# Where output copies stand in VectorE's queue, and where a norm's factor is applied

## The chip, the cores and the metric

The kernel runs on one core of a Trainium2 chip. The metric is device time in microseconds (us). TensorE multiplies matrices into PSUM, VectorE (DVE) and ScalarE (ACT) do elementwise work and read PSUM, GpSimd (POOL) issues the indirect fetches here, and SyncE (SP) issues the other transfers. Each engine takes its own instructions in order, and engines wait for one another through semaphores.

## The reference, cut to what matters

256 tokens of 1024 channels go through two blocks, in fp32. The first has a convolution, a differential attention and a cross attention; the second has stick-breaking attention and a gated recurrence, and ends in an expert layer. The change touches the seam before that layer, and the layer's end:

```python
h = rms_norm_2(x, norm_ffn)                 # x * rsqrt(mean(x*x) + eps) * g
q = h @ w_query                             # 1024 -> 8 heads x 2 x 128
s = q . sub_keys                            # 128 keys for each half
top_s, top_i = top_k(s, 16)                 # then the best 16 of 16 x 16 sums
g = softmax(best_s);  u, v = expert_u[idx], expert_v[idx]
act = gelu(h . u)
x = x + sum(g * act * v)                    # 16384 experts, 8 x 16 of them for a token
```

## The kernel before, in words

Channels lie on partitions, tokens along the row; activations are tiles of 128 x 8 x 256. The weights of all layers but the experts come as 94 blocks, each in two halves of 128x1024 fp32 (0.524 MB). ACT casts a half to a high part and VectorE subtracts to get a low part, and `linT` adds three products: high weight by high activation, high by low, low by high. Activations are split into a high and a low tile (`split`, or `gain_col`, which multiplies with the gain on the way).

The queries of the expert layer need the normalised residual. Its mean square is summed on TensorE with `rms_sq` as the last parts of the residual `xr` come (L922 to L927); `rstd_of` makes the token's factor `rx` on ACT and VectorE; `rms_cols` (L963) writes `h3f` = xr times gain times factor, column by column, and splits it into `h3`. Eight `linT` (L1066) then make the queries, ACT copies each out of PSUM (L1068), and small products with the keys give the scores. VectorE finds the top 16 in a background list of small steps (`top16`, `decode`, `gates`), which ends with the indices of the rows to gather.

The expert layer is done in two ways. For 160 tokens all 16384 experts are multiplied: the weights u (`u_pair`, L288) and then v (`v_pair`, L1169) stream through, 128 halves each, and one-hot products (L1136, L1147) set the gates in between. The sums y stand in four PSUM tiles `yT` until the end. For the other 96 tokens only the chosen rows are fetched: 96 fetches of 128 rows of u, then 96 of v (`fetch`, L1178, 0.524 MB each), on GpSimd's queue. VectorE multiplies rows of u with the token (`dot`, L1185) and sums rows of v into `acc` (`axpy`, L1203). A fetch needs a free buffer: three of the tag `gat` and five of `gat2`. Fetch `n` takes a `gat` buffer if `n % 8 < 3`. The weights u and v go through a ring of 13 halves on SP's queue (L230).

At the end `rows_out` transposes and adds the gathered tokens' parts (L1229, L1231), copies them out (L1233) into a `gat` buffer and stores them (L1234). For the 160 tokens ACT and VectorE copy `yT` (L1282, L1283) and SP stores it (L1284).

The program is traced in Python, and a planner lays the instructions of each engine in an order by a time model of its own; the code's order is a priority only. `issue_after(x)` lays the instructions in its block behind x in the same engine's queue. The order that came out is that of the profile.

Of the kernel before, what the change touches and what calls it, by code (L numbers as in the profile page):

```python
# [188 lines left out]
def build(tc, xT, memT, vec, con, con0, wcat, rgw, keysT, u, v, urow, vrow, out):  # L189
    nc = tc.nc  # L190
    es = ExitStack()
    with es:
        cpool = es.enter_context(tc.tile_pool(name="const", bufs=1))
        spool = es.enter_context(tc.tile_pool(name="stream", bufs=1))
        ex = ExitStack()
        xpool = ex.enter_context(tc.tile_pool(name="xres", bufs=1))

# [11 lines left out]
        def V(n, i=0, k=1):  # L209
            o, _ = VEC[n]  # L210
            return VT[:, o + i:o + i + k]
# [135 lines left out]
        xr = xpool.tile([P, NC, T], F32, name="xr")  # L347
        rx = xpool.tile([P, T], F32, name="rx")
        cur = {}
# [9 lines left out]
        def statp():  # L359
            return cur["ps"].tile([P, 512], F32, name="stat", tag="stat", bufs=1)  # L360
# [64 lines left out]
        def bc2(r):  # L425
            return r.unsqueeze(1).to_broadcast([P, 2, T])
# [37 lines left out]
        with ExitStack() as e1:  # L464
            big = e1.enter_context(tc.tile_pool(name="big", bufs=11, side="right"))
            cur["sm"] = e1.enter_context(tc.tile_pool(name="sm", bufs=2, side="right"))
# [4 lines left out]
            def bigt(n, dt=F32):  # L471
                return big.tile([P, NC, T], dt, name=n, tag="big")


# [13 lines left out]
            nc.sync.dma_start(ident, con0[:, :P])  # L488
            mgh, mgl = bigt("mgh", F32R), bigt("mgl", F32R)
            for c in range(NC):  # L490
# [109 lines left out]
            qd, kd, vd = bigt("qd"), bigt("kd"), big.tile([P, 2, 1024], F32, name="vd", tag="big")  # L600
            oxh, oxl = bigt("oxh", F32R), bigt("oxl", F32R)
            for j in range(4):
# [63 lines left out]

            odh, odl = bigt("odh", F32R), bigt("odl", F32R)
            for j in range(4):
# [46 lines left out]
            with tc.issue_after(last.ins):  # L715
                for c in range(NC):
                    nc.scalar.activation(cn[:, c], cn[:, c], AF.Silu, bias=V("conv_ln_b", c))
            ch, cl = bigt("ch", F32R), bigt("cl", F32R)
            for j in range(4):
# [10 lines left out]

            h2 = (bigt("h2h", F32R), bigt("h2l", F32R))
            st = statp()
# [185 lines left out]
            hold = state["rstd"]  # L918
            st2 = statp()
            for j in range(2):  # L920
                for k, ps in enumerate(linK(mx, 0, None if j else (scp(), scp()))):
                    sl = slice(4 * j + 2 * k, 4 * j + 2 * k + 2)  # L922
                    g = smt("gate", 512, 3).rearrange("p (a b) -> p a b", a=2)
                    nc.vector.tensor_mul(g, ps, bc2(rsb))  # L924
                    nc.vector.tensor_add(xr[:, sl], xr[:, sl], g)
                    rms_sq(xr, st2, 4 * j + 2 * k, NC)
                state["hold"] = hold  # L927
            rstd_of(st2[:, :T], 1.0 / 1024, T, out=rx)

# [18 lines left out]

        NB, MORE = 3, 5
        xG = rows.tile([P, NC, NG], F32, name="xG")  # L950
# [8 lines left out]
        with ExitStack() as e3:  # L959
            hq = e3.enter_context(tc.tile_pool(name="hq", bufs=1, side="right", reuse_waits="tile"))  # L960
            h3 = [hq.tile([P, NC, T], F32R, name="h3hi"), hq.tile([P, NC, T], F32R, name="h3lo")]
            rms_cols(xr, "norm_ffn_2", *h3, r=rx, full=h3f)
            state["hold"] = state["split"]  # L963
            ex.close()
# [100 lines left out]
            for hd in range(8):  # L1065
                pq = linT(h3, hd == 0)  # L1066
                q = tk.tile([P, 2, T], F32, name="q", bufs=1)
                nc.scalar.copy(q, pq)  # L1068
                pss = gps.tile([P, 512], F32, name="gp", tag="gp").rearrange("p (t h n) -> p t h n", t=2, h=2)
                for t in range(2):  # L1070
                    for p_ in range(2):
                        nc.tensor.matmul(pss[:, t, p_], q[:, p_, t * P:(t + 1) * P], kT[:, 2 * hd + p_],
                                         start=True, stop=True)
                ss = tk.tile([P, 2, 2, P], F32, name="ss", bufs=2)
                nc.scalar.copy(ss, pss)
                for t in range(2):
                    for p_ in range(2):
                        top16(V16[:, t, hd, p_], I16[:, t, hd, p_], ss[:, t, p_], "s2")
                    bg.append((0.0, cands(hd, t)))
                background(2.5)  # L1080
# [91 lines left out]
            def fetch(src, k):  # L1172
                n, box["slot"] = box["slot"], box["slot"] + 1
                if "more" in box and n % (NB + MORE) >= NB:
                    g = box["more"].tile([P, 1024], F32, name="gat2", bufs=MORE)
                else:
                    g = rows.tile([P, 1024], F32, name="gat", tag="gat", bufs=NB)
                nc.gpsimd.indirect_dma_start(g, None, src, bass.IndirectOffsetOnAxis(gi[:, 0, k:k + 1].bitcast(U32), 0))  # L1178
                return g
# [17 lines left out]
            def axpy(k, m, g):  # L1197
                with tc.issue_after(state["dve"].ins):
                    if m not in acc:
                        acc[m] = rows.tile([P, 1024], F32, name=f"acc{m}", tag=f"row{m}")  # L1200
                        nc.vector.tensor_scalar_mul(acc[m], g, cG[:, k:k + 1])
                    else:
                        nc.vector.scalar_tensor_tensor(acc[m], g, cG[:, k:k + 1], acc[m], op0=ALU.mult, op1=ALU.add)  # L1203

            def gathered():

                held = []
                for f, src in ((dot, urow), (axpy, vrow)):
                    for m, (o_, g, _) in enumerate(groups):
                        for k in range(o_, o_ + g):  # L1210
                            if len(held) == NB + ("more" in box) * MORE:
                                fn, *a = held.pop(0)
                                fn(*a)
                            a = (k, hrow[m]) if f is dot else (k, m)
                            held.append((f, *a, fetch(src, k)))
                            weights()
                            yield
                for fn, *a in held:
                    fn(*a)
                yield  # L1220
# [35 lines left out]
        ga.append(g2pool.tile([P, 32, D], F32, name="ga2"))  # L1256
        box["more"] = es.enter_context(tc.tile_pool(name="rows2", bufs=1, side="right", reuse_waits="tile"))
        for g8 in range(D // 8):
# [21 lines left out]
        for b in range(4):  # L1280
            o = ga[0][:, 2 * b:2 * b + 2]
            nc.scalar.copy(o[:, 0], yT[b][:, 0, :D])  # L1282
            nc.vector.tensor_copy(o[:, 1], yT[b][:, 1, :D])  # L1283
            nc.sync.dma_start(yo[:, 2 * b:2 * b + 2], o)  # L1284
# [22 lines left out]
```

## Time and profile before

| | |
|---|---|
| median of 3 runs | 1322.68 us (1321.14 to 1325.76) |
| profiled execution | 1325.82 us, its span 1324.0 us |
| TensorE busy | 1250.4 us, 94% |
| VectorE busy | 937.6 us, 71% |
| ScalarE busy | 456.7 us, 34% |
| GpSimd busy | 218.3 us, 16% |
| moved by DMA | 340.75 MB, mean 257 GB/s |

The span is the time from the first to the last instruction. Busy shares are means over stages with different limits. TensorE's matmuls are pipelined, and a busy TensorE can still be fed slowly.

### The profile page before, as it was taken

How to read it: one execution, taken by the hardware profiler on the slowest of the kernel's cores; microseconds unless marked ns; L12 is line 12 of the kernel's file. 1: busy time of each engine (PE TensorE's matmuls, PEld its weight loads, DVE VectorE, ACT ScalarE, POOL GpSimd, SP SyncE). 2: the span in 40 equal slices, each digit the busy share in tenths (PEclk: the TensorE clock that was granted, in tenths of full speed). 3: DMA queues.
4: the chain of work that ended last, by engine and by line, in shares of the span. 5: the costliest groups of instructions: out<-in, count | busy, mean ns of one | idle time of the engine just before them, and what ended most of it. 6: DMA issues, size and time to landing. Idle time of an engine off the chain costs nothing.

```text
span 1324.0 us, 24472 instructions
## 1 busy us (share of the span) xinstructions
PE 1250.4 (94%) x9948; PEld 1211.4 (91%) x9948; DVE 937.6 (71%) x1806; ACT 456.7 (34%) x733; POOL 218.3 (16%) x222
## 2 busy tenths in 40 slices
PE   8999999999999999998999999999999999999902
PEld 7999999899999999887999999999999999999901
DVE  6799888888997687847998544875547865440095
ACT  7546677668647458845313010000100000000000
POOL 0000000000000000000012532323412253330072
PEclk9999999999999999999999999999999999999955
DMA  8555543444565564324676999999999999999384
GB/s 293 191 191 178 164 133 120 131 139 156 161 194 174 177 203 137 124 75 157 207 260 205 410 409 408 409 388 384 379 339 353 366 384 409 409 409 409 142 334 189
DMA packets 94864, 340.75 MB, mean 257 GB/s; under 512 B 10576, under 2 KB 12048, under 8 KB 94624
## 3 DMA queue, kind: packets, MB, share of 16 engines
q1 hardware_dynamic: 66752, 237.98, 50.8%
q0 software_dynamic: 28000, 101.22, 19.9%
q8 instruction: 78, 1.28, 0.4%
q14 instruction: 34, 0.28, 0.1%
HBM read 338.01 MB, written 1.05 MB: 256 GB/s over the span
## 4 chain that ended last, share of the span: by engine, by line
PE 78%; DMA 6%; DVE 6%; issue 5%; ACT 3%; POOL 1%; POOLq 0%; SPq 0%; ACTq 0%
PE lin L288 18%; PE y L1169 15%; PE lin L308 10%; PE lin L307 10%; PE lin L309 10%; DMA w<-in_v 6%; PE gp L1136 1%; PE lin L341 1%; PE lin L343 1%; PE lin L342 1%; POOL gat L1178 1%; PE stat L459 1%; ACT whi L247 1%; DVE I L989 1%; PE sc L840 1%
## 5 line engine op out<-in xcount | busy, mean ns | idle before, releaser
L288 PE MATMUL lin<-h3f,w 128*128 128x160 f32 x2048 | 290.6, 302 | 1.8 <-issue 1.8
L1169 PE MATMUL y<-ga,w 128*128 128x160 f32 x2048 | 287.3, 301 | 1.0 <-issue 0.5
L288 PEld LDWEIGHTS lin<-h3f,w 128*128 128x128 f32 x2048 | 281.3, 191 | 3.0 <-issue 2.8
L1169 PEld LDWEIGHTS y<-ga,w 128*128 128x128 f32 x2048 | 279.4, 190 | 3.5 <-issue 1.8
L248 DVE TENSOR_TENSOR wlo<-raw,whi 128x1024 fp32r<-128x1024 f32 x188 | 229.4, 1223 | 64.3 <-ACT whi L247 63.4
L247 ACT CAST whi<-raw 128x1024 fp32r<-128x1024 f32 x188 | 196.2, 1049 | 167.7 <-PE lin L308 124.9
L308 PE MATMUL lin<-hl,whi 128*128 128x256 f32 x704 | 200.4, 285 | 0.0
L309 PE MATMUL lin<-hh,wlo 128*128 128x256 f32 x704 | 200.0, 284 | 0.0
L307 PE MATMUL lin<-hh,whi 128*128 128x256 f32 x704 | 199.9, 284 | 0.0
L1203 DVE SCALAR_TENSOR_TENSOR acc<-gat,cG,acc 128x1024 f32<-128x1024 f32 x94 | 120.8, 1285 | 55.7 <-DMA gat<-in_vrow,gi 54.1
L1185 DVE CUSTOM_DVE_ANT_0 gat<-gat,hrow 128x1024 f32<-128x1024 f32 x96 | 116.1, 1223 | 33.0 <-DMA gat<-in_urow,gi 32.9
L1178 POOL DMA_INDIRECT gat<-in_urow,gi x96 | 105.3, 1097 | 200.1 <-DVE sG L1185 187.4
L309 PEld LDWEIGHTS lin<-hh,wlo 128*128 128x128 f32 x704 | 132.7, 189 | 2.2 <-issue 1.9
L308 PEld LDWEIGHTS lin<-hl,whi 128*128 128x128 f32 x704 | 132.8, 189 | 1.7 <-issue 1.4
L307 PEld LDWEIGHTS lin<-hh,whi 128*128 128x128 f32 x704 | 132.6, 188 | 1.4 <-issue 1.0
L1178 POOL DMA_INDIRECT gat<-in_vrow,gi x96 | 96.9, 1009 | 181.2 <-DVE acc L1203 71.4
L1158 ACT ACTIVATE ga<-lin 128x320 f32<-128x320 f32 x64 | 28.0, 437 | 243.6 <-PE lin L288 230.5
L535 DVE SCALAR_TENSOR_TENSOR cacc<-ub,VT,cacc 128x256 f32<-128x256 f32 x240 | 103.9, 479 | 0.0
L955 POOL DMA_DIRECT2D fold<-in_con x1 | 0.7, 701 | 595.9 <-DVE gate L924 595.9
L1147 DVE SCALAR_TENSOR_TENSOR ga<-gp,ga 128x256 f32<-128x256 f32 (+1 forms) x60 | 29.1, 511 | 79.3 <-PE gp L1136 54.9
L1282 ACT COPY ga<-y 128x160 f32<-128x160 f32 x4 | 1.2, 292 | 206.9 <-PE y L1169 206.9
L1283 DVE COPY ga<-y 128x160 f32<-128x160 f32 x4 | 1.2, 320 | 68.7 <-ACT ga L1282 68.7
(372 smaller groups left out, 2135.2 us busy)
## 6 DMA issues: line engine op xcount, KB each, us to landing
raw<-in_wcat SPq DMA_DIRECT2D x188, 512.0 KB
w<-in_u SPq DMA_DIRECT2D x128, 512.0 KB
w<-in_v SPq DMA_DIRECT2D x128, 512.0 KB
gat<-in_urow,gi POOLq DMA_INDIRECT x96
gat<-in_vrow,gi POOLq DMA_INDIRECT x96
m_t<-in_memT SPq DMA_DIRECT2D x4, 256.0 KB
xr<-in_xT SPq DMA_DIRECT2D x2, 512.0 KB
kT<-in_keysT SPq DMA_DIRECT2D x1, 1024.0 KB
```

What stands on the lines that cost most here:

```text
L247: nc.scalar.copy(h, raw)
L248: state["sub"] = nc.vector.tensor_sub(l, raw, h.bitcast(F32))
L288: nc.tensor.matmul(ps[:, a], ws[a][:, c * P:(c + 1) * P], x[:, c], start=c == 0, stop=c == 7)
L307: nc.tensor.matmul(ps[:, a], wh, ah[:, c], start=(a, c) in first, stop=False)
L308: nc.tensor.matmul(ps[:, a], wh, al[:, c], start=False, stop=False)
L309: nc.tensor.matmul(ps[:, a], wl, ah[:, c], start=False, stop=(a, c) in last)
L535: nc.vector.scalar_tensor_tensor(cacc[:, c], s, w, cacc[:, c], op0=ALU.mult, op1=ALU.add)
L1147: state["dve"] = nc.vector.scalar_tensor_tensor(g_[:, :, tl], p_, 1.0 / GSCALE, g_[:, :, tl], op0=ALU.mult, op1=ALU.mult)
L1169: nc.tensor.matmul(yT[c // 2][:, c % 2, :D], ws[a][:, c * P:(c + 1) * P], g[:, a], start=False, stop=i == 63 and (a, c % 2) == (1, 1))
L1178: nc.gpsimd.indirect_dma_start(g, None, src, bass.IndirectOffsetOnAxis(gi[:, 0, k:k + 1].bitcast(U32), 0))
L1185: nc.vector.tensor_tensor_reduce(out=g, in0=g, in1=h, scale=1.0, scalar=0.0, op0=ALU.mult, op1=ALU.add, accum_out=sG[:, k:k + 1])
L1203: nc.vector.scalar_tensor_tensor(acc[m], g, cG[:, k:k + 1], acc[m], op0=ALU.mult, op1=ALU.add)
```

## The change

Three edits. First, the queries are made from the residual times the gain, before the factor is known: `gain_col` writes `h3` as each part of `xr` comes, and VectorE multiplies the token's factor `rk` onto the product as it leaves PSUM; `h3f` is still made, for the expert products. Second, the split pairs `mg`, `ox`, `od`, `c`, `h2` and `h3` share two fixed tiles in a pool `hq` that lives to the end; the ring `big` has 9 tiles in place of 11, and the extra fetch buffers become four halves of those two tiles, so that the fetch ring has 7 buffers. Third, the VectorE copies of the output are laid behind the last sum of gathered rows.

```diff
+        hpool = es.enter_context(tc.tile_pool(name="hq", bufs=1))
-        rx = xpool.tile([P, T], F32, name="rx")
+        rx = rk = hpool.tile([P, T], F32, name="rx")
-            big = e1.enter_context(tc.tile_pool(name="big", bufs=11, side="right"))
+            big = e1.enter_context(tc.tile_pool(name="big", bufs=9, side="right"))
+            def pair(n):
+                return [hpool.tile([P, NC, T], F32R, name=n + x, tag=x) for x in "hl"]
-            mgh, mgl = bigt("mgh", F32R), bigt("mgl", F32R)
+            mgh, mgl = pair("mg")
...
-            h2 = (bigt("h2h", F32R), bigt("h2l", F32R))
+            h2 = pair("h2")
+            h3 = pair("h3")
             for j in range(2):
                 for k, ps in enumerate(linK(mx, 0, None if j else (scp(), scp()))):
...
                     nc.vector.tensor_add(xr[:, sl], xr[:, sl], g)
+                    for c in range(sl.start, sl.stop):
+                        gain_col(xr, "norm_ffn_2", *h3, c)
                     rms_sq(xr, st2, 4 * j + 2 * k, NC)
-            rstd_of(st2[:, :T], 1.0 / 1024, T, out=rx)
+            rstd_of(st2[:, :T], 1.0 / 1024, T, out=rk)
-        NB, MORE = 3, 5
+        NB, MORE = 3, 4
-            rms_cols(xr, "norm_ffn_2", *h3, r=rx, full=h3f)
-            state["hold"] = state["split"]
+            for c in range(NC):
+                nc.vector.scalar_tensor_tensor(h3f[:, c], xr[:, c], V("norm_ffn_2", c), rk, op0=ALU.mult, op1=ALU.mult)
-                pq = linT(h3, hd == 0)
+                pq = linT(h3)
-                nc.scalar.copy(q, pq)
+                nc.vector.tensor_mul(q, pq, bc2(rk))
-                if "more" in box and n % (NB + MORE) >= NB:
-                    g = box["more"].tile([P, 1024], F32, name="gat2", bufs=MORE)
+                j = n % (NB + MORE) - NB
+                if j >= 0:
+                    if j % 2 == 0:
+                        box["two"] = hpool.tile([P, 2, 1024], F32, name="gat2", tag="hl"[j // 2])
+                    g = box["two"][:, j % 2]
-                        nc.vector.scalar_tensor_tensor(acc[m], g, cG[:, k:k + 1], acc[m], op0=ALU.mult, op1=ALU.add)
+                        state["sum"] = nc.vector.scalar_tensor_tensor(acc[m], g, cG[:, k:k + 1], acc[m], op0=ALU.mult, op1=ALU.add)
-                            if len(held) == NB + ("more" in box) * MORE:
+                            if len(held) == NB + MORE:
-        box["more"] = es.enter_context(tc.tile_pool(name="rows2", bufs=1, side="right", reuse_waits="tile"))
-            nc.vector.tensor_copy(o[:, 1], yT[b][:, 1, :D])
+            with tc.issue_after(state["sum"].ins):
+                nc.vector.tensor_copy(o[:, 1], yT[b][:, 1, :D])
```

## Rows read from the trace of the kernel before

**Rows 1.** The page's slices, 33.1 us each.
```profile
DVE  6799888888997687847998544875547865440095
GB/s 293 191 191 178 164 133 120 131 139 156 161 194 174 177 203 137 124 75 157 207 260 205 410 409 408 409 388 384 379 339 353 366 384 409 409 409 409 142 334 189
```

**Rows 2.** Timeline of the end: start, duration, instruction [idle before, releaser].
```profile
1258.20 0.33 DVE L1283 COPY ga<-y 128x160 f32<-128x160 f32 x1 [68.70 <-ACT ga L1282]
1258.56 3.74 SPq L1284 DMA_DIRECT2D out<-ga  x4
1259.99 1.98 POOL L1178 DMA_INDIRECT gat<-in_vrow,gi  x1 [69.28 <-DVE ga L1283]
1261.53 48.82 DVE L1203 SCALAR_TENSOR_TENSOR acc<-gat,cG,acc 128x1024 f32<-128x1024 f32 x37
1300.91 1.02 POOL L1178 DMA_INDIRECT gat<-in_vrow,gi  x1 [0.30 <-issue]
1301.14 1.05 ACT L1233 COPY gat<-lin 32x512 f32<-32x512 f32 x2 [40.47 <-DVE acc L1203]
1301.77 3.53 PE L1229 MATMUL lin<-ident,xG 128*64 128x128 f32 x16 [41.48 <-issue]
1310.41 3.68 PE L1231 MATMUL lin<-acc,fold 128*64 128x512 f32 x4 [5.11 <-DVE acc L1203]
```

**Rows 3.** Timeline of VectorE and GpSimd, the last before 1190 us.
```profile
1185.67 1.28 DVE L1203 SCALAR_TENSOR_TENSOR acc<-gat,cG,acc 128x1024 f32<-128x1024 f32 x1 [1.28 <-DMA gat<-in_vrow,gi]
1188.22 1.28 DVE L1203 SCALAR_TENSOR_TENSOR acc<-gat,cG,acc 128x1024 f32<-128x1024 f32 x1 [1.26 <-DMA gat<-in_vrow,gi]
...
1189.77 0.94 POOL L1178 DMA_INDIRECT gat<-in_vrow,gi  x1 [1.60 <-DVE acc L1203]
```

**Rows 4.** Windows: length, busy us (count) of each engine, clock, DMA share, GB/s.
```profile
960.00:1000.00 40.00, 40.00 (x352) 38.88 (x351) 21.02 (x46) 0.78 (x3) 8.28 (x8) 1.00 0.94 346
1120.00:1160.00 40.00, 40.00 (x297) 40.00 (x296) 19.17 (x16) 0.00 (x0) 15.07 (x16) 1.00 1.03 409
1189.50:1235.00 45.50, 45.06 (x324) 43.79 (x323) 0.00 (x1) 0.00 (x0) 0.94 (x1) 1.00 1.03 409
1235.00:1258.00 23.00, 23.00 (x172) 23.00 (x171) 0.00 (x0) 0.12 (x1) 0.00 (x0) 1.00 0.06 21
```

**Rows 5.** Timeline of the seam before the queries.
```profile
596.82 1.23 ACT L437 ACTIVATE sq<-xr 128x512 f32<-128x512 f32 x2 [3.83 <-DVE xr L925]
599.58 0.63 ACT L437 ACTIVATE sq<-xr 128x512 f32<-128x512 f32 x1 [0.23 <-PE stat L439]
601.23 2.34 PE L946 MATMUL y<-xr,ident 128*128 128x160 f32 x16
604.72 3.18 ACT L384 CAST h3hi<-h3f 128x256 fp32r<-128x256 f32 x8 [1.47 <-DVE h3f L407]
605.18 0.38 PE L307 MATMUL lin<-h3hi,whi 128*128 128x256 f32 x1 [1.61 <-ACT h3hi L384]
607.38 2.76 DVE L384 TENSOR_TENSOR h3lo<-h3f,h3hi 128x256 fp32r<-128x256 f32 x8
607.85 0.39 PE L308 MATMUL lin<-h3lo,whi 128*128 128x256 f32 x1 [2.29 <-DVE h3lo L384]
```

**Rows 6.** Windows of TensorE alone behind the seam: busy, granted clock, DMA.
```profile
609.00:610.00 1.00, 1.00 (x7) 0.50 0.74 157
612.00:613.00 1.00, 1.00 (x10) 0.95 0.14 57
```

**Rows 7.** Lines L924 and L413: count, min/median/max ns, first and last start.
```profile
L924 DVE TENSOR_TENSOR gate<-lin,rs x2: 686/688/689, 595.5 to 597.9; 128x512 f32<-128x512 f32 x2
L413 DVE SCALAR_TENSOR_TENSOR h2l<-xr,VT,h2h x8: 479/480/484, 466.8 to 480.7; 128x256 fp32r<-128x256 f32 x8
```

**Rows 8.** A window of the background list on VectorE.
```profile
660.00:680.00 20.00, 20.00 (x153) 20.00 (x152) 19.74 (x111) 4.69 (x8) 2.47 (x4) 1.00 0.84 281
```

**Rows 9.** Timeline of GpSimd: the first gather.
```profile
721.77 1.84 POOL L1178 DMA_INDIRECT gat<-in_urow,gi  x1 [3.36 <-DMA gi<-pk]
```

More of the change, by code (lines that the diff above doesn't have):

```diff
@@ L600, in build @@
             qd, kd, vd = bigt("qd"), bigt("kd"), big.tile([P, 2, 1024], F32, name="vd", tag="big")
-            oxh, oxl = bigt("oxh", F32R), bigt("oxl", F32R)
+            oxh, oxl = pair("ox")
             for j in range(4):
@@ L665, in gated @@
                 return i
-            odh, odl = bigt("odh", F32R), bigt("odl", F32R)
+            odh, odl = pair("od")
             for j in range(4):
@@ L717, in build @@
                     nc.scalar.activation(cn[:, c], cn[:, c], AF.Silu, bias=V("conv_ln_b", c))
-            ch, cl = bigt("ch", F32R), bigt("cl", F32R)
+            ch, cl = pair("c")
             for j in range(4):
@@ L959, in build @@
         with ExitStack() as e3:
-            hq = e3.enter_context(tc.tile_pool(name="hq", bufs=1, side="right", reuse_waits="tile"))
-            h3 = [hq.tile([P, NC, T], F32R, name="h3hi"), hq.tile([P, NC, T], F32R, name="h3lo")]
-            rms_cols(xr, "norm_ffn_2", *h3, r=rx, full=h3f)
-            state["hold"] = state["split"]
+            for c in range(NC):
+                nc.vector.scalar_tensor_tensor(h3f[:, c], xr[:, c], V("norm_ffn_2", c), rk, op0=ALU.mult, op1=ALU.mult)
             ex.close()
```

## The prediction

> **What bounds the kernel now.** I read the page's slices first [rows 1]. From slice 22 (728 us) on the DMA moves 339 to 410 GB/s, until slice 37, where it falls to 142 while VectorE has done nothing for two slices; then it runs again at 334. Idle DMA in the middle of a DMA-bound stretch, with an engine asleep beside it, is what the reader should look for. The timeline of the end says why [rows 2]. VectorE's next instruction at 1189.5 us is the first copy of the finished output out of PSUM (L1283); it stands there 68.7 us, until TensorE finishes y. Behind it in the same queue are 39 sums of gathered rows (L1203). GpSimd can fetch a further row only when a sum has freed its buffer, so its next fetch waits 69.3 us for that copy. When y is done, two of the sums slip in between copies and the other 37 follow at 48.82/37 = 1.32 us each; the last ends at 1310.4, and the span ends 13.6 us later.
>
> What flowed before the stall is in the next view [rows 3]: sums start 2.56 us apart, each ended by a row's landing, which is 0.524 MB/2.56 us = 205 GB/s, half of the 409 GB/s that the window from 1120 to 1160 shows [rows 4]. The gathers and the weights v share the DMA evenly. In the stall the weights have it alone: 409 GB/s up to 1235, then 21 [rows 4].
>
> **The change, part by part.** *Output copies behind the last sum.* The four L1283 copies now follow the last L1203. To find when that sum ends I count bytes, since the DMA is the limit. From 1189.5 to 1235 it moved 409 x 45.5 = 18.6 MB, to 1258 another 21 x 23 = 0.5 MB. Left over after 1258 are 31 row fetches (the first and the last are in [rows 2]) of 0.524 MB: 16.25 MB. Together 35.4 MB; at 409 GB/s 86.5 us, so the last row lands at 1276.0. Of the 19.1 MB, eight rows (the outstanding ones) are 4.2 MB and some 28 are weight halves. Shared evenly, 28 halves take 28 x 2.56 = 72 us, to 1261.5; TensorE ends y some 2.3 us later, near 1264 instead of 1260. In that time 28 of the 39 rows are summed; the other 11 run alone at 1.32 us: 1276. Both ways agree. With one sum behind the landing it ends near 1277.6, against 1310.4: **32.8 us** earlier. The four copies then take 4 x 0.32 us and SP's four output transfers 3.7 us from first to last issue, as in [rows 2]. That is less than the chain of the gathered rows' own output, and runs beside it: SP's queue is empty by then, and nothing else waits on it.
>
> The split need not be even. If gathers got more, y would end up to 14 us later, at about 1278, and its copies, issues and landing would end near 1292, where the other chain ends too; if they got less, the last rows would be limited by their 1.32 us. The sum of bytes stays, so I keep 1276, with 2 us either way.
>
> *Ring of seven.* Before, the last three rows sat in the five extra buffers, so an output buffer for the first 32 rows became free seven sums before the end, at 1301.1 (L1233) [rows 2]. With fetch number modulo 7 the three "gat" buffers hold the last three rows. That output copy starts only at the third last sum's end, 2.64 us before the last. The 16 matmuls of L1229, which wait for those copies' PSUM, start at 0.6 us after it and take 3.5 us, so they end 1.5 us after the last sum, and L1231 stands behind them: **+1.5 us** (nothing if a warm TensorE does them at twice the speed).
>
> One buffer fewer, and pairs that are freed together, mean that five to seven rows are outstanding in place of eight. In the saturated stretches five rows still are 5 x 2.56 = 12.8 us of queue, so the DMA does not run dry: nothing. Between 860 and 1080 the DMA is not saturated (346 GB/s at 960 to 1000 [rows 4]); there the rows wait for VectorE's order, in which the one-hot products stand between the sums. A planner that sees a smaller ring may put fewer sums between these products. No row shows that. Below, nothing; above, 10% of the some 110 rows used by then (96 of u, and the 57 sums done at 1189.5 less the 43 that 2.56 us apiece put behind 1080), 11 x 1.28 = 14 us of DMA. I take **+2 us**, near the lower end, since buffers are refilled at once and stand full there.
>
> *Queries from the residual.* Removed from the path: TensorE ends the ident products at 603.6 (L946), waits for the factor and the normalised columns, does one matmul at 605.18, and waits again, for the low halves, until 607.85 [rows 5]; then it runs at 1.2 GHz, granted 0.50, from 609 to past 612 [rows 6], which costs 1.6 us. Now h3's halves come from xr itself. Added ahead of the statistics: eight ACT casts (0.40 us, by eight in 3.18 us [rows 5]) and eight VectorE subtractions at 0.48 us, the row of the same helper at L413 [rows 7]. From the first square at 596.82 on, ACT then has 4 x 0.63 + 3.18 = 5.7 us of work, to 602.5; now its last square ends at 600.2, so the statistics and the factor may come 2.3 us later. If TensorE takes everything in its present order, the ident products end at 605.5 and the queries gain 2.4 us and the clock's 1.6; if it takes the ident products and the first columns while it waits, up to 6; if the clock falls all the same, 2.4. I take **4**.
>
> VectorE pays: eight products of PSUM with the factor, 128x512, at 0.686 us (L924 on PSUM is the same shape) = 5.5 us, in place of ACT's copies [rows 7], and at most 8 x (0.48 - 0.345) = 1.1 us for the low halves, which took 2.76 us together. VectorE is full from 620 to 720 (19.74 of 20 us [rows 8]), and the first gather (721.77 [rows 9]) waits for that list. Its idle time ahead of 620 is some 7 us, which an earlier first query can fill. The first gather thus moves between 0.4 us earlier and 6.6 later; I take 2 later. A microsecond there is worth under half of one at the end: the DMA moves 205 to 260 GB/s in these slices [rows 1], so about half of its time is unused. TensorE's 4 us fetch weights earlier at the 224 GB/s that these slices average, and give back 4 x 224/409 = 2.2. Against that stand 2 x 0.45 = 0.9. Net: **-1.3 us** (-5 to +5).
>
> *Split halves in fixed tiles.* mg, ox, od, c, h2 and h3 take turns in two tiles, the big ring falls from 11 to 9: eleven in all, as before. Each pair is dead before the next is written, with at least one linT (5.6 us) between: nothing; if one write waited, some 5 us once.
>
> *Sum:* -32.8 + 1.5 + 2 - 1.3 = -30.6. On the profiled execution, span 1324.0 and 1325.82 in all: span 1293.4, time 1295.2. That execution is 3.1 us above the median of the runs, 1322.68; taken from the median, **1292 us**.
>
> **A rule weighed.** The rows give 409 GB/s, with both streams in it, for 45 us and longer [rows 4]. The Trainium skill, "DMA: Bandwidth & Descriptors", section Specifications, gives a core's share of HBM as about 358 GB/s; by it the 35.4 MB would take 99 us and the gain shrink by about 12 us. The trace disagrees, and the sum goes by the trace.
>
> **The rivals.**
> 1. *The order fills better.* Between 840 and 1080 the DMA leaves about 9 MB unused (slices 25 to 32 [rows 1]), 22 us. If VectorE's new order recovers half of it: 1281. For: any new plan reorders these; against: nothing in the change aims there. 0.10.
> 2. *Later gathers.* The first gather 6.6 us late, or 11 rows fewer before 1080: 10 to 15 us of the gain go, 1302 to 1307. For: VectorE has no room at 620 to 720. 0.15.
> 3. *The copies' place is not what holds the sums,* or the same bytes come back as a wait for weights: 1319 to 1326. The bytes speak against it: the DMA is nearly idle from 1235 to 1258 while 31 fetches wait. 0.03.
> 4. *Slower: the paired buffers.* A fetch into a pair's first half waits for the row after its own too. With 192 rows there are 27 rounds of seven; if each round left the DMA dry for L, 27 L is lost, and from L = 1.2 us (33/27) nothing is left; at 2 us 1345. For: rows freed two at a time. Against: 12.8 us of queue remains. 0.03.
> 5. *The slower pipe.* Both streams from 1190 on at the 346 GB/s of 960 to 1000: 35.4 MB take 102 us, 16 more, and the time is 1308. That would need the rate to fall in a mix that ran at 409 from 1120 to 1160. 0.01. The page's limit, above, is the rule that would make it so; the trace does not bear it out.
>
> **How the numbers follow.** The forecast holds 0.68, in 1284 to 1300: the split, the tail's 1.5 and the query's ends. The better order takes the range down to 1281, the later gathers up to 1306; outside lie the far parts of rivals 1 and 2, and rivals 3 to 5. About 0.3% (4 us) is what a measurement can tell from no change. Every case but 3 and 4 is faster: 0.94; rival 3 is the 0.03 of no change, rival 4 the 0.03 of slower.
>
> **What would show it.** Right: no idle of tens of us before L1283; L1203 starts 2.56 us apart until about 1260 and 1.32 after; the slices at 409 GB/s up to the last one or two; y's last matmul near 1264; the output copy of the first 32 rows within 3 us of the last sum; L1068 on VectorE near 0.69 us; the first query matmul near 604 and no half clock behind it. Wrong: gathers that start past 728, more unused DMA from 860 to 1080 than 22 us' worth, POOL waits at each pair, or L1231 in TensorE's queue ahead of the last products with v.

## The result, and the profile after

The changed kernel takes 1303.2 us, median of 3 runs (1302.02 to 1305.13), against 1322.68: a ratio of 0.9851, with an interval of 0.9817 to 0.9885. It is faster by 19.5 us, where 30.6 us were forecast; 1303.2 lies inside the whole range, up to 1306, but outside the 1284 to 1300 of the likeliest case and beside the second rival ("later gathers", 1302 to 1307). The profiled execution took 1303.2 us with a span of 1301.2, where the sum gave 1293.4: 7.8 us too few.

The page's slices of the changed kernel, 32.5 us each:

```profile
DVE  6889888888997777846999754778348775444465
GB/s 292 187 192 180 162 145 115 130 128 146 157 202 164 209 179 146 150 80 97 192 271 216 303 409 409 409 407 352 387 350 342 363 365 409 409 409 409 409 391 203
```

The two empty slices of VectorE and the hole of 142 GB/s beside them [rows 1] are gone: from slice 33 the DMA runs at 409 GB/s to slice 37. What is left at the front is slice 22 at 303 (715.7 to 748 us; the gathers start in it, at 729), and slices 26 to 32, which still leave DMA unused: 297 GB/s short of 409 in sum, times 32.5 us, is 23.6 us at 409 GB/s; before it was 270 and 21.9 us [rows 1].

The timeline of its end: start, duration, instruction, idle before and releaser.

```profile
1258.40 0.94 POOL L1187 DMA_INDIRECT gat<-in_vrow,gi  x1 [4.18 <-DVE acc L1212]
1259.40 1.28 DVE L1212 SCALAR_TENSOR_TENSOR acc<-gat,cG,acc 128x1024 f32<-128x1024 f32 x1 [1.27 <-DMA gat<-in_vrow,gi]
1261.25 3.53 PE L1175 MATMUL y<-ga,w 128*128 128x160 f32 x24 [1.19 <-DMA w<-in_v]
1261.61 10.53 DVE L1212 SCALAR_TENSOR_TENSOR acc<-gat,cG,acc 128x1024 f32<-128x1024 f32 x8 [0.92 <-DMA gat<-in_vrow,gi]
...
1283.05 3.95 DVE L1212 SCALAR_TENSOR_TENSOR acc<-gat,cG,acc 128x1024 f32<-128x1024 f32 x3 [0.21 <-DMA gat<-in_vrow,gi]
1284.36 1.05 ACT L1242 COPY gat<-lin 32x512 f32<-32x512 f32 x2 [19.26 <-DVE acc L1212]
1284.99 3.67 PE L1238 MATMUL lin<-ident,xG 128*64 128x128 f32 x16 [20.22 <-ACT gat L1242]
...
1286.91 1.01 DVE L1292 COPY ga<-y 128x160 f32<-128x160 f32 x4
1287.26 1.99 SPq L1293 DMA_DIRECT2D out<-ga  x4
1288.46 2.79 PE L1240 MATMUL lin<-acc,fold 128*64 128x512 f32 x4
```

Read it beside [rows 2]. The sums start 2.56 us apart up to 1259.40, each ended by a row's landing; TensorE ends y at 1264.8 (forecast near 1264); the four output copies stand behind the last sum and SP issues their transfers at once. But from 1261.61 on there are still 18 sums to do (8, then 2, 4 and 1 in the lines left out, then 3), to 1287.0, where the forecast had 11 left. Seven rows at the 1.32 us of a row alone are 9.2 us, the order of the 9.4 us that the last sum is late. The row of GpSimd shows the ring and its pairs: this fetch, into the first half of a pair, waited 4.18 us for a sum; a fetch of the kernel before waited 1.60 [rows 3].

Where were the rows lost? Counted from the starts of the VectorE instructions that use them (L1185, L1201 and L1203 in before, L1194, L1210 and L1212 after; L1201 and L1210 are the first sum of each group of tokens), rows used up to a time in us:

```
             800  880  960  1080  1120  1189
before        28   49   73   109   126   153
after         26   45   68   104   120   147
```

Two are missing at once, as the gathers start at 729.37 in place of 721.77 [rows 9]; three more follow by 960 and one by 1120, and from there on both kernels use them at the same pace. So the rows are lost ahead of the stretch that the copies' edit touches. Rows are not all of it: what the gathers leave, the weights can take. The time of the DMA that goes unused, counted further below, tells more.

The seam of the changed kernel, in order of time:

```profile
597.37 1.21 DVE L249 TENSOR_TENSOR wlo<-raw,whi 128x1024 fp32r<-128x1024 f32 x1
599.70 1.22 DVE L249 TENSOR_TENSOR wlo<-raw,whi 128x1024 fp32r<-128x1024 f32 x1
602.04 1.22 DVE L249 TENSOR_TENSOR wlo<-raw,whi 128x1024 fp32r<-128x1024 f32 x1
603.81 0.58 PE L308 MATMUL lin<-h3h,whi 128*128 128x256 f32 x2
611.35 0.47 ACT L375 ACTIVATE rv<-stat,VT 128x256 f32<-128x256 f32 x1 [3.05 <-PE stat L440]
614.46 0.42 DVE L381 SCALAR_TENSOR_TENSOR rx<-rt,rs 128x256 f32<-128x256 f32 x1
614.92 1.28 DVE L969 SCALAR_TENSOR_TENSOR h3f<-xr,VT,rx 128x256 f32<-128x256 f32 x3
729.37 1.05 POOL L1187 DMA_INDIRECT gat<-in_urow,gi  x1 [3.72 <-DMA gi<-pk]
```

The first query matmul starts at 603.81 (forecast near 604; before, steadily from 607.85 [rows 5]), and no half clock follows: the window from 609 to 610 has TensorE busy throughout at a granted 1.00, against 0.50 in [rows 6].

```profile
609.00:610.00 1.00, 1.00 (x11) 1.00 (x10) 0.00 (x0) 0.00 (x0) 0.00 (x0) 1.00 0.00 0
1189.50:1235.00 45.50, 44.33 (x297) 40.15 (x296) 22.53 (x18) 0.00 (x0) 21.51 (x18) 1.00 1.03 409
1235.00:1258.00 23.00, 21.92 (x146) 19.75 (x145) 11.52 (x10) 0.00 (x0) 9.38 (x8) 1.00 1.03 409
1258.00:1280.00 22.00, 5.48 (x37) 4.75 (x35) 18.32 (x16) 1.17 (x4) 16.28 (x14) 0.77 0.95 351
```

But the factor's last step, which before starts at 603.74, starts at 614.46. Of these 10.7 us, 3.0 come from ahead of the seam (the first part of the residual, L924 and L930, starts at 593.17 before and 596.17 after). For the rest, TensorE has taken query matmuls ahead of the last statistics (ACT waits for them to 611.35), and three low parts of weights (L249) stand between the residual's parts on VectorE. TensorE's early start does not last: its last query matmul ends at 661.30, against 660.30 before. The products with the factor are then as forecast: L1074 takes 0.680 us (median of 8) in place of the estimated 0.686.

What sets the first gather is VectorE's work. These are windows of VectorE alone (length, busy time and count, clock, DMA share, GB/s) from the first part of the residual to the first indices of the rows to gather, in before and in the changed kernel:

```profile
593.17:714.46 121.29, 111.42 (x455) 0.99 0.62 202
596.17:721.71 125.54, 116.70 (x467) 1.00 0.62 206
```

VectorE has 5.3 us more to do, and its idle time shrinks by 1.0 only (9.9 to 8.8), so the indices come 4.3 us later than the start of the seam explains.

The same windows [rows 4] show the hole filled: 409 GB/s from 1235 to 1258, where it was 21, and 351 from 1258 to 1280, where after y's end rows come alone.

### The profile page after: what moved, and what is told of

The parts are those of the page before. It is cut to its first block, busy times and chain, and to the rows that moved or that the text cites. A ratio compares the mean times of both kernels' runs of the same rounds, so it can differ in the third digit from the quotient of the medians.

```text
span 1301.2 us, 24424 instructions
## 1 busy us (share of the span) xinstructions
PE 1251.8 (96%) x9948; PEld 1211.0 (93%) x9948; DVE 943.4 (72%) x1814; ACT 452.4 (35%) x725; POOL 239.4 (18%) x222
## 4 chain that ended last, share of the span: by engine, by line
PE 57%; DMA 17%; DVE 10%; issue 9%; POOL 4%; ACT 3%; SPq 0%; POOLq 0%; DVEq 0%; ACTq 0%
DMA gat<-in_vrow,gi 14%; PE lin L289 14%; PE lin L308 10%; PE lin L309 10%; PE lin L310 10%; POOL gat L1187 4%; DMA gat<-in_urow,gi 2%; PE lin L342 1%; PE lin L344 1%; PE lin L343 1%; DVE acc L1212 1%; PE gp L1142 1%; ACT whi L248 1%; DVE wlo L249 1%; PE stat L460 1%
## 5 line engine op out<-in xcount | busy, mean ns | idle before, releaser
L289 PE MATMUL lin<-h3f,w 128*128 128x160 f32 x2048 | 285.6, 300 | 1.7 <-ACT ga L1164 1.7
L249 DVE TENSOR_TENSOR wlo<-raw,whi 128x1024 fp32r<-128x1024 f32 x188 | 229.2, 1221 | 68.7 <-ACT whi L248 67.8
L1212 DVE SCALAR_TENSOR_TENSOR acc<-gat,cG,acc 128x1024 f32<-128x1024 f32 x94 | 120.8, 1285 | 99.3 <-DMA gat<-in_vrow,gi 97.4
L1194 DVE CUSTOM_DVE_ANT_0 gat<-gat,hrow 128x1024 f32<-128x1024 f32 x96 | 116.3, 1221 | 42.8 <-DMA gat<-in_urow,gi 42.8
L1187 POOL DMA_INDIRECT gat<-in_urow,gi x96 | 107.5, 1120 | 214.2 <-DVE sG L1194 188.2
L1187 POOL DMA_INDIRECT gat<-in_vrow,gi x96 | 113.8, 1186 | 119.3 <-DVE acc L1212 87.0
L1203 ACT ACTIVATE cG<-sG 128x16 f32<-128x16 f32 x6 | 1.3, 212 | 110.9 <-DVE sG L1194 110.9
```

The source lines that it names most:

```text
L249: state["sub"] = nc.vector.tensor_sub(l, raw, h.bitcast(F32))
L289: nc.tensor.matmul(ps[:, a], ws[a][:, c * P:(c + 1) * P], x[:, c], start=c == 0, stop=c == 7)
L1194: nc.vector.tensor_tensor_reduce(out=g, in0=g, in1=h, scale=1.0, scalar=0.0, op0=ALU.mult, op1=ALU.add, accum_out=sG[:, k:k + 1])
L1212: state["sum"] = nc.vector.scalar_tensor_tensor(acc[m], g, cG[:, k:k + 1], acc[m], op0=ALU.mult, op1=ALU.add)
```

## The experiments

The theory to be tested is the prediction's: the copies alone are worth some 33 us, and the other edits nearly nothing (+2.2 together). The rivals: the others cost some 10 us, by the ring of seven, by the queries, or by the order in which VectorE's one-hot products stand among the rows. "Rows ahead of the last one-hot product" is 99 in before and 93 in the changed kernel. Each ratio below is to the kernel before on the same chip: one chip for e1, e2, e3 and e7, another for e5, e6, e8 and e9, a third for e10 to e13. Runs of different chips are compared by these ratios.

**e1, the copies alone.** Before, with its copies behind the last sum; the ring of eight, the queries and the tiles stay.

```diff
-                        nc.vector.scalar_tensor_tensor(acc[m], ...)
+                        state["sum"] = nc.vector.scalar_tensor_tensor(acc[m], ...)
...
-            nc.vector.tensor_copy(o[:, 1], yT[b][:, 1, :D])
+            with tc.issue_after(state["sum"].ins):
+                nc.vector.tensor_copy(o[:, 1], yT[b][:, 1, :D])
```

> The kernel before with the third edit alone: the four VectorE copies of the output behind the last sum; everything else is in the order of before. Theory A (the copies are worth what the sum of bytes said, and the other two edits took 12 us of it back): last sum near 1277.6, no longer tail, span 1291, time 1290 against 1322.7, ratio 0.975. Theory B (the sum of bytes was too large, the other edits are neutral): 1303, ratio 0.985.

Measured: 1293.81 us, 0.9782 (0.9758 to 0.9806), span 1291.0. The end of its timeline:

```profile
1263.54 1.28 DVE L1203 SCALAR_TENSOR_TENSOR acc<-gat,cG,acc 128x1024 f32<-128x1024 f32 x1 [0.15 <-DMA gat<-in_vrow,gi]
1265.50 11.85 DVE L1203 SCALAR_TENSOR_TENSOR acc<-gat,cG,acc 128x1024 f32<-128x1024 f32 x9 [0.68 <-DMA gat<-in_vrow,gi]
1268.14 1.05 ACT L1233 COPY gat<-lin 32x512 f32<-32x512 f32 x2
1277.27 1.01 DVE L1284 COPY ga<-y 128x160 f32<-128x160 f32 x4
1277.41 3.67 PE L1231 MATMUL lin<-acc,fold 128*64 128x512 f32 x4 [6.68 <-DVE acc L1203]
```

The last sum ends at 1277.35 (forecast 1277.6), 33.0 us earlier than before. Nine sums are left at 1265.50, and all of them run without a gap. Its median is the lowest of all versions, and its interval lies below the changed kernel's.

**e2, everything but the copies.** The changed kernel with the copies where they were.

```diff
-            with tc.issue_after(state["sum"].ins):
-                nc.vector.tensor_copy(o[:, 1], yT[b][:, 1, :D])
+            nc.vector.tensor_copy(o[:, 1], yT[b][:, 1, :D])
```

> The changed kernel with the copies where they were: edits one and two alone, the rest of each queue as in the changed kernel. Theory A: slower than before by some 12 us, 1335. Theory B: 1323, no change. Either way VectorE should stand tens of us at the first copy, as before.

Measured: 1342.95 us, 1.0135 (1.0114 to 1.0156), span 1345.6. Without the copies' edit the rest of the change makes the kernel slower. Its timeline has before's stall, and longer, 75.85 us against 68.70 [rows 2]:

```profile
1258.26 0.33 DVE L1291 COPY ga<-y 128x160 f32<-128x160 f32 x1 [75.85 <-ACT ga L1290]
```

Only 142 rows are used by 1189, eleven fewer than before, and each row that is left runs alone after the stall; the last sum ends at 1331.13. So the rest of the change costs 0.0135, 17.9 us, with the stall, and 0.0069, 9.1 us, without it: the parts do not simply add, since a row that is missing before the stall comes back at 1.32 us.

**e3, the queries undone.** The changed kernel with before's `rms_cols` and ACT copies of the product; ring, pairs, tiles and copies stay.

```diff
-                    for c in range(sl.start, sl.stop):
-                        gain_col(xr, "norm_ffn_2", *h3, c)
...
+            rms_cols(xr, "norm_ffn_2", *h3, r=rk, full=h3f)
+            state["hold"] = state["split"]
...
-                nc.vector.tensor_mul(q, pq, bc2(rk))
+                nc.scalar.copy(q, pq)
```

> The changed kernel with the queries made from the normalised columns again, split after the factor, copied by ACT; fixed tiles, ring of seven and copies stay. Theory A1 (the loss came from the seam: VectorE's added products and the later factor put the first gather 4.6 us later than the part before the seam explains): first gather near 725, time 1298. Theory A2 (the loss came from the ring of seven and its pairs): within 2 us of 1303, whatever the first gather does.

Measured: 1301.38 us, 0.983 (0.9815 to 0.9846); first gather at 723.27, last sum at 1285.54. The gathers start 6.1 us earlier than in the changed kernel, and the time is 0.0021 lower, 2.8 us, within the intervals. So the queries cost little, and most of what is missing is in the ring, the pairs and the tiles: e3 against e1, on the same chip, is 7.6 us longer in medians, 0.0048 by the ratios. Theory A2 comes nearer than A1.

**e5, a ring of seven single buffers**, on e1.

```diff
-        NB, MORE = 3, 5
+        NB, MORE = 3, 4
```

> Copies alone (1293.8), with one fetch buffer fewer: three and four single ones. Theory R (the ring's size and its pairs took the 7.6 us that lie between copies alone and the changed kernel with the queries undone): the output buffer of the first 32 rows still becomes free late (+1.5), and a share of the rest, 1296 to 1299. Theory P (it is the pairs): 1295.5, only the tail's 1.5. Theory S (it is the fixed tiles and the stages ahead of the seam, 3 us later): 1295.5.

Measured: 1300.62 us, 0.9826 (0.9811 to 0.984), an interval just above e1's (0.9758 to 0.9806); span 1298.3. The end:

```profile
1262.94 21.10 DVE L1203 SCALAR_TENSOR_TENSOR acc<-gat,cG,acc 128x1024 f32<-128x1024 f32 x16 [0.62 <-DMA gat<-in_vrow,gi]
1281.43 1.05 ACT L1233 COPY gat<-lin 32x512 f32<-32x512 f32 x2 [15.22 <-DMA gat<-in_vrow,gi]
1285.53 2.87 PE L1231 MATMUL lin<-acc,fold 128*64 128x512 f32 x4
```

One number changed takes 0.0044, some 5.8 us, of e1's gain, with an interval of some 2 to 9.5 us. Against e8 below, which ran on the same chip with eight buffers and e1's copies, it is 3.7 us longer in medians. Sixteen sums are left at 1262.94, and the last ends at 1284.04, 6.7 us after e1's. Part of that is not the ring: this run's first gather starts at 724.28, 2.5 us after e1's, and 1.95 us of that stand already ahead of the seam (594.69 against 592.74), in code that both share. The forecast's tail is here too: the output copy of the first 32 rows starts at the third last sum's end, L1231 1.49 us after the last sum, but it takes 2.87 us in place of 3.67.

**e6, seven buffers, four of them as two pairs**, on e1: the changed kernel's ring, without its other edits.

```diff
-        NB, MORE = 3, 5
+        NB, MORE = 3, 4
...
+                j = n % (NB + MORE) - NB
+                if j >= 0:
+                    if j % 2 == 0:
+                        box["two"] = box["more"].tile([P, 2, 1024], F32, name="gat2", tag="hl"[j // 2])
+                    g = box["two"][:, j % 2]
```

> Copies alone, with three single buffers and two pairs, each pair one tile that is freed when both its rows are summed; the pool is the one of the extra buffers before. Theory P (the pairs cost): 1299 to 1301, with waits of some us at GpSimd's fetch into each pair's first half, and gaps in VectorE's sums once the weights are through. Theory S: 1295.5.

Measured: 1302.33 us, 0.9837 (0.9822 to 0.9852), 0.0011 above e5 and within its interval. The pairs' wait is there: between 720 and 1200 us GpSimd waits 7 us or longer nine times (97.6 us in all), against three times (35.8) in e5 and four (49.3) in e1. It costs some 1.5 us, which is not separable from nothing.

**e8, the fixed tiles of the first stage alone**, on e1.

```diff
-            big = e1.enter_context(tc.tile_pool(name="big", bufs=11, side="right"))
+            big = e1.enter_context(tc.tile_pool(name="big", bufs=9, side="right"))
+            fx = e1.enter_context(tc.tile_pool(name="fx", bufs=1, side="right"))
...
+            def pair(n):
+                return [fx.tile([P, NC, T], F32R, name=n + x, tag=x) for x in "hl"]
```

> Copies alone, with mg, ox, od, c and h2 in two fixed tiles and a ring of nine in the first stage; nothing changed from the expert layer on, eight fetch buffers. Theory S: the stages ahead of the seam end 3 us later, 1297 to 1299. Theory P or R: 1294, no change.

Measured: 1296.96 us, 0.98 (0.9787 to 0.9813), overlapping e1's. The first gather starts at 721.93, as in before (721.77), so the stages ahead of the seam did not end later, and Theory S fails in its reason though its time, 1297, came out. The last sum ends at 1280.65, 29.7 us earlier than before and 3.3 later than in e1. At least part of this lies in code that e8, e1 and before share: between 800 and 960 us e1 moved 400 GB/s, e8 395 and before 393. Told as time of the DMA, such differences can be compared over all runs. The table has GB/s in three stretches, and in brackets the time in us that the DMA left unused there, taken against 409 GB/s:

| | 720 to 800 | 800 to 960 | 960 to 1080 | unused in all | last sum ends |
|---|---|---|---|---|---|
| before | 392 (3.3) | 393 (6.3) | 355 (15.8) | 25.4 | 1310.4 |
| e1, eight buffers | 394 (2.9) | 400 (3.5) | 355 (15.8) | 22.3 | 1277.4 |
| e8, eight buffers | 393 (3.1) | 395 (5.5) | 356 (15.6) | 24.2 | 1280.7 |
| e5, seven | 389 (3.9) | 390 (7.4) | 356 (15.6) | 26.9 | 1284.0 |
| e6, seven, pairs | 392 (3.3) | 390 (7.4) | 352 (16.7) | 27.5 | 1284.3 |
| e3, seven, pairs | 389 (3.9) | 393 (6.3) | 351 (17.0) | 27.2 | 1285.5 |
| changed kernel | 379 (5.9) | 391 (7.0) | 352 (16.7) | 29.6 | 1287.0 |

Where the copies stand behind the last sum, it ends the later, on the whole, the more the DMA has left unused by 1080: 7.3 us more in the changed kernel than in e1, and the last sum 9.6 later. One execution of each kernel was profiled, and kernels with eight buffers differ by 3 us among themselves.

**e7, the held casts behind the residual's factor**, on the changed kernel: it gives `hold` back its place behind the factor.

```diff
             rstd_of(st2[:, :T], 1.0 / 1024, T, out=rk)
+            state["hold"] = state["rstd"]
```

> The changed kernel with one line: the casts of the second query block are laid behind the factor in place of behind the factor before it. In the changed kernel two of them stand among the residual's parts on VectorE and ACT. Theory A1: the residual's last part comes 2.4 us earlier, the factor and the first gather too, time 1301. Rival: TensorE then waits for the second query's weights, the query stage takes the 2.4 us back, 1303 or more.

Measured: 1300.54 us, 0.9833 (0.9813 to 0.9853); first gather at 726.86, 2.5 us earlier. Of these, 1.2 us stand ahead of the seam (594.94 against 596.17), so the casts account for some 1.3 us of the later gathers; the time moves less than the intervals tell apart.

**e9, eight buffers in the changed kernel**, on e7: four single ones and the two pairs.

```diff
-        NB, MORE = 3, 4
+        NB, MORE = 4, 4
```

> The changed kernel with the casts behind the factor (1300.5) and four single buffers in place of three, so eight in all, four of them in pairs. If the ring's size counts: 1297. If the pairs count: 1300, no change.

Measured: 1301.41 us, 0.9825 (0.9812 to 0.9839): no change from e7. The first gather (728.35) is 1.5 us later than in e7, and 97 rows stand ahead of the last one-hot product, against 94. A ring as large as before's, half of it in pairs, gives nothing back. It does show in the rows: 45 are used from 800 to 960, as in before, against 42 in e7. But the weights lose what the rows gain: the DMA moves 383 GB/s in that stretch, against 387, and y ends at 1272.6, against 1263.4.

**e10 to e13, the order of rows and one-hot products.** One theory said that a smaller ring makes the planner put fewer rows between the one-hot products, as the forecast's "fewer rows" had it. Each of these lays every product behind a given row.

```diff
+                    need = min(ROWS[blk * 20 + g8], len(rowins))
+                    with tc.issue_after(rowins[need - 1].ins):
                     for g_, p_ in parts:
                         state["dve"] = nc.vector.scalar_tensor_tensor(...)
```

In e10 (on e5) and e11 (on the changed kernel) the rows are before's, 99 ahead of the last product; in e12 (on e1) and e13 (on the changed kernel) a product goes behind every row traced before it, 116 and 117.

> Seven single fetch buffers with the copies behind the last sum (1300.6), with each one-hot product laid behind the row that stands before it in VectorE's order of before: 99 rows ahead of the last product in place of 95. Theory O (the planner's order takes the time, the ring itself does not): 1295 to 1296, what is left being the tail's 0.6 us and the chance of the start. Theory G (a ring of seven starves the DMA as it runs): 1300, no change.

> The changed kernel (1303.2) with the same lower bounds, 99 rows ahead of the last product in place of 93. Theory O: 6 rows at 1.28 us come back, 1296 to 1297. Theory G, or the loss lies in the late first gather: 1301 to 1303.

> Copies alone (1293.8) with each one-hot product laid behind every row that the code has traced by then: 116 rows ahead of the last product in place of 99. The DMA leaves 7.9 MB unused between 840 and 1080, 15 rows. Theory O: these fill, the last sum comes up to 15 x 1.28 us earlier, 1277 to 1284. Rival: products that wait for rows hold TensorE, which then waits for PSUM or for gates: 1294 or more.

> The changed kernel with the same edit, 117 rows ahead of the last product in place of 93. Theory O: 1280 to 1287, within 4 us of the run before it, its first gather being 7 us late. Theory G: the ring of seven and its pairs keep it 7 us or more behind that run.

Measured: e10 1300.41 us, 0.9819 (0.9802 to 0.9837), no change from e5; e11 1310.23, 0.9891 (0.9872 to 0.9909), 0.0040 above the changed kernel (0.9817 to 0.9885), with 97 rows used by 1080 against its 104; e12 1297.2, 0.9793 (0.9775 to 0.981), no gain on e1; e13 1326.75, 1.0018 (1.0007 to 1.0029). Theory O fails in all four. The groups of VectorE's lines from 720 to 1120 say why; they end with busy time, mean, and the idle time before with its releasers. First e5, then e10:

```profile
L1147 DVE SCALAR_TENSOR_TENSOR ga<-gp,ga 128x256 f32<-128x256 f32 (+1 forms) x60 | 29.0, 510 | 56.3 <-PE gp L1136 50.5 <-ACT ga L1158 5.2
L1127 DVE TENSOR_TENSOR A<-io,idxT 128x1024 f16<-128x1024 f16 x40 | 27.2, 681 | 6.4 <-PE gp L1136 6.4
```

```profile
L1149 DVE SCALAR_TENSOR_TENSOR ga<-gp,ga 128x256 f32<-128x256 f32 (+1 forms) x60 | 28.8, 506 | 18.6 <-PE gp L1136 13.4 <-ACT ga L1160 5.2
L1127 DVE TENSOR_TENSOR A<-io,idxT 128x1024 f16<-128x1024 f16 x40 | 27.6, 690 | 46.7 <-PE gp L1136 46.4 <-issue 0.2
```

The wait for TensorE's one-hot matmuls left the product (50.5 us to 13.4) and came back at the next comparison (6.4 to 46.4): VectorE waits for TensorE in either place, and 106 rows are used by 1080 in both. In e13 the forced rows go too far: TensorE, the other side of the same exchange, now waits for VectorE, and the weights come more slowly.

```profile
1120.00:1160.00 40.00, 20.08 (x169) 19.30 (x170) 35.34 (x51) 0.00 (x0) 24.88 (x20) 0.62 0.78 257
```

Its window from 1120 to 1160 has TensorE busy 20.08 of 40 us and the DMA at 257 GB/s, against 40.00 and 409 before [rows 4].

## Why the prediction came near, and where it was short

**What bounded the kernel, and the copies: right in the mechanism, some 4 us too large.** The hole was the copies' wait: it went with them in e1 and came back in e2. Counting bytes at 409 GB/s gave its worth as 32.8 us; e1's last sum ends 33.0 us earlier, and its span is 33.0 shorter. That this meets the forecast so closely is in part luck. In medians e1 gains 29.6 us and by its ratio 28.8, since before's profiled execution, from which the sum was made, stood 3.1 us above its median; and e1's own profiled execution left 3.1 us less of the DMA unused from 720 to 1080 than before, ahead of anything that the edit touches. The share between the streams was even as assumed, and y ended within a microsecond of the forecast in the changed kernel (1267.7 in e1). One step in the count was too hopeful: rows that come alone do not fill the DMA, which from 1258 to 1280 moved 351 GB/s in the changed kernel, not 409.

The slower pipe, rival 5's 346 GB/s, is excluded: the changed kernel's windows from 1189.5 to 1258 moved 409 in both parts. The Trainium skill, "DMA: Bandwidth & Descriptors", section Specifications, gives about 358 GB/s for a core's share of HBM; it did not limit this kernel, which runs on one core.

**The rest of the change: mis-sized.** The other edits together were to cost 2.2 us (+1.5 +2 -1.3). They cost 0.9851 - 0.9782 = 0.0069 of 1322.68, 9.1 us, and by the two intervals at least 3.6. By terms:

- *Ring of seven.* Forecast +3.5, of it +2 for the rows "near the lower end, since buffers are refilled at once and stand full there". e5 measured 3.7 us against e8 and 5.8 against e1, so the forecast lies at the lower end of what was measured, and no run shows it wrong by itself. The tail's part was right in its mechanism (L1240 starts 1.46 us after the last sum) and smaller in size: the clock granted from 1288.4 to 1291.3, right behind 16 matmuls, is 0.68, against 0.50 for the same four matmuls in e1, so they take 2.79 us in place of 3.67, and the tail grows by 0.6 us (13.6 to 14.2). The exception that the prediction named was another one: the 16 matmuls themselves were to run at twice the speed, and they took 3.67 us. The rows are the larger part: e5 uses 148 by 1189, against 153, one of them missing already at 800, where its later first gather shows. Whatever the order, 40 to 42 rows are used from 800 to 960 in every run with seven buffers on the way from e1 to the changed kernel (e5, e6, e3, e7, e10 and the changed kernel), against 45 or 46 in before, e1 and e8.
- *Pairs.* Forecast nothing outside rival 4. Rival 4's waits exist, but cost some 1.5 us in e6, not separable from nothing, and not the 33 that would have undone the gain.
- *Queries: the step that the trace contradicts.* Forecast -1.3; the changed kernel against e3 gives some +2.8 by the ratios and +1.8 by the medians, not separable from nothing nor from the forecast. TensorE's start was right (603.81, no half clock), and so was the price of the products. But of the 4 us that TensorE was to gain, its last query matmul shows 2.0 when the 3.0 us ahead of the seam are taken off, and none in the time itself. And VectorE's idle time ahead of 620, "some 7 us, which an earlier first query can fill", took up 1.0 us of its 5.3 us of added work. The factor explains it: "may come 2.3 us later" was too little, it came 10.7 later, 7.7 of it from the seam itself, since TensorE took query matmuls ahead of the statistics, and casts of the next weights were no longer held back behind this factor; and no product of a query can be made before it. In e7, where it starts 4.6 us earlier, VectorE's idle time in the same stretch is 7.1 us in place of 8.8. So the first gather came 7.6 us late, 4.6 of it from the seam (forecast 2, at most 6.6), and the DMA left 5.9 us unused from 720 to 800, against 3.9 in e3 and 2.9 in e1. The delay ahead of the seam changes from kernel to kernel without a pattern that was found (3.0 us here, 1.5 in e5, none in e8 and in e10), so it is scatter between builds or executions as far as is known.
- *Fixed tiles.* Nothing forecast, nothing separable measured (e8).

So the likeliest case held for the hole, and rival 2 for the number: its 11 rows fewer by 1080 were 5, its gathers 6.6 us late were 7.6. Of the 11 us by which the median fell short of the forecast, some 4 are the copies' size and some 7 the other edits'.

**What stays open.** How the 9.1 us divide between ring, pairs and queries: each piece is about as large as its interval. And why a ring of seven uses fewer rows. The planner's order, as the forecast had it, is not upheld: forced back, it gave nothing (e10) or made it worse (e11), and more rows between the products gave nothing either (e12). That it is the ring's size as the kernel runs fits the rows from 800 to 960, in e9 too, but e9's time gives nothing back; half of its buffers were in pairs, and eight single ones in the changed kernel were not tried, so size and pairing aren't told apart there.

## What to carry to other kernels

A copy that must wait for the end of one stream should not stand, in an in-order queue, ahead of work that frees another stream's transfer buffers; what it costs is the bytes left over, divided by the rate that the DMA has shown with both streams running. Take an edit of several parts apart: here two lines were worth more than the whole, and the buffer given up to make room for the rest cost some 3.5 to 6 us. An operation pulled ahead of a factor also pulls ahead whatever was held behind that factor, so list what is released by the earlier event, and who now stands behind it. And take the size of an effect from several runs: one profiled execution met the forecast within 0.2 us here, and the medians were 4 us away.

## What the runs showed of the hardware

Rows fetched alone at the end don't all come at the 1.32 us that the forecast took from [rows 2]: the changed kernel's last 18 sums take 25.4 us from 1261.61 on, 1.41 each, with four gaps in which VectorE waits for a row, though the DMA moves only 351 GB/s from 1258 to 1280; e1's last nine take 11.85 us, 1.32 each, without one. The trace points to GpSimd's issues and not to the ring: from 1265.34 on each fetch is issued 0.30 us after the one before it has ended, without a wait for a buffer, most of them 1.32 us apart, but the one at 1273.27 takes 1.86 us and the one at 1276.75 1.18, in place of 1.02. No run changed it. And with 16 small matmuls right ahead of them, the four last ones took 0.9 us less, at a granted clock of 0.68 in place of 0.50.
